# Binary cross-entropy on one core: loading the next predictions ahead of the store

## Chip, cores and metric

The kernel runs on one core of a Trainium2 chip. The metric is device time in microseconds. Three runs of the kernel before took 1864.36, 1864.77 and 1865.55 us; the median is 1864.77.

## What is computed

```python
def reference(pred, target):          # both 8192 x 8192 float32
    eps = 1e-7
    pred = np.clip(pred, eps, 1 - eps)
    return -(target * np.log(pred) + (1 - target) * np.log(1 - pred))
```

The targets are 0 or 1, drawn as integers and kept as float32. So each output is -ln(pred) where the target is 1 and -ln(1 - pred) where it is 0. Every element is independent. 268.44 MB of predictions and as many of targets are read, and 268.44 MB are written.

## The kernel before

With targets of 0 or 1 the two logarithms are one: |target - 1 + pred| is pred where the target is 1 and 1 - pred where it is 0. A chunk of w columns on 128 partitions therefore takes these steps, in place on one buffer of predictions:

- `clip` (line 88, VectorE): bound the predictions to [eps, 1 - eps].
- `log` (lines 94, 97, 98): VectorE computes (target - 1) + pred, ScalarE takes the absolute value (97) and then the logarithm (98).
- `back` (line 102, VectorE): multiply by -1.
- `load_p` (line 72) and `load_t` (line 75) are the loads of predictions and targets, `store` (line 79) writes the result.

The work is cut into 40 chunks: two of 5120 columns at the start (0 and 1), 35 of 14336 columns (2 to 36), two of 5632 and one of 1024 at the end (37 to 39, called a, b and c). Predictions live in a ring of three slots of 14336 columns: chunks 0 and 1 share the first slot, chunk 2 has the second, chunk 3 the third, chunk 4 the first again, and so on. So the load of predictions k+2 overwrites the slot from which store k-1 reads, and has to wait until that store has landed. (Predictions 3 are the first of the third slot and wait for nothing; predictions 4 wait for stores 0 and 1.) Targets are turned from float32 to bfloat16 by the load and live in one single buffer, so the load of targets k+1 waits until VectorE has read the last of targets k (line 94, second half). Chunk c has places of its own in both buffers.

The order of the instructions on each engine is the written one; there is no scheduler. Chunks 2 to 36 are computed in two halves. VectorE's order in a round of chunk k is clip and line 94 of the first half, the same of the second half, then `back` of both halves; each `back` waits for ScalarE.

All loads but that of predictions 0, and all stores but the last three chunks', are issued by GpSimd (POOL) and go through one queue. An instruction that waits on POOL holds up all that is behind it. In a round of the middle POOL issues targets k+1 (line 75), store k (line 79) and predictions k+2 (line 72), in this order. The start issues targets 0 and 1 and predictions 1 and 2 with no wait, predictions 0 come by ScalarE's queue; the stores of a, b and c go by SyncE's queue.

Of the kernel before, what the change touches and what calls it, by code (L numbers as in the profile page):

```python
# [1 line left out]

# [4 lines left out]

EPS = 1e-7

BIG = 14 * 1024  # L10
FIRST = 5 * 1024
LAST = 5632
TAIL = 1024
SLOTS = 3


def plan(total):
    n = (total - 2 * FIRST - 2 * LAST - TAIL) // BIG
    assert n > 4 and total == 2 * FIRST + n * BIG + 2 * LAST + TAIL
    spots = [(FIRST, 0, 0), (FIRST, FIRST, FIRST)]  # L20
    spots += [(BIG, k % SLOTS * BIG, 0) for k in range(1, n + 1)]
    end = (n + 1) % SLOTS * BIG
    spots += [(LAST, end, 0), (LAST, end + LAST, LAST)]
    return spots + [(TAIL, SLOTS * BIG, BIG)]


@with_exitstack
def kernel(
    ctx: ExitStack,
    tc: tile.TileContext,  # L30
    pred: bass.AP,
    target: bass.AP,
    out: bass.AP,
):
    nc = tc.nc
    fp32 = mybir.dt.float32
    bf16 = mybir.dt.bfloat16
    Alu = mybir.AluOpType
    Act = mybir.ActivationFunctionType
    P = nc.NUM_PARTITIONS  # L40

    R, C = pred.shape
    spots = plan(R * C // P)
    n = len(spots)
    widths = [s[0] for s in spots]
    cols = [sum(widths[:k]) for k in range(n)]

    def chunk(ap, k):
        flat = ap.rearrange("r c -> (r c)")
        return flat[cols[k] * P : (cols[k] + widths[k]) * P].rearrange("(p w) -> p w", p=P)  # L50

    pool = ctx.enter_context(tc.tile_pool(name="rings", bufs=1))
    ring_p = pool.tile([P, SLOTS * BIG + TAIL], fp32, name="ring_p", tag="ring_p")
    ring_t = pool.tile([P, BIG + TAIL], bf16, name="ring_t", tag="ring_t")
    warm = pool.tile([1, 8], fp32, name="warm", tag="warm")

    def spot(k, part=(0, 1)):
        w, c, _ = spots[k]
        i, m = part
        return ring_p[:, c + i * w // m : c + (i + 1) * w // m]  # L60

    def spot_t(k, part=(0, 1)):
        w, _, c = spots[k]
        i, m = part
        return ring_t[:, c + i * w // m : c + (i + 1) * w // m]

    def load_p(k):
        if k == 0:
            for rows in (slice(0, P, 2), slice(1, P, 2)):
                nc.scalar.dma_start(out=spot(0)[rows], in_=chunk(pred, 0)[rows])  # L70
        else:
            nc.gpsimd.dma_start(out=spot(k), in_=chunk(pred, k))  # L72

    def load_t(k):
        nc.gpsimd.dma_start(out=spot_t(k), in_=chunk(target, k))  # L75

    def store(k):
        queue = nc.sync if k >= n - 3 else nc.gpsimd
        queue.dma_start(out=chunk(out, k), in_=spot(k))  # L79

    def store_rows(k):
        src, dst = spot(k), chunk(out, k)
        for first, last in ((0, 108), (108, 120), (120, 128)):
            nc.sync.dma_start(out=dst[first:last], in_=src[first:last])

    def clip(k, *part):
        p = spot(k, *part)
        nc.vector.tensor_scalar(  # L88
            out=p, in0=p, scalar1=EPS, scalar2=1 - EPS, op0=Alu.max, op1=Alu.min
        )  # L90

    def log(k, *part):
        p = spot(k, *part)
        nc.vector.scalar_tensor_tensor(  # L94
            out=p, in0=spot_t(k, *part), scalar=1.0, in1=p, op0=Alu.subtract, op1=Alu.add
        )
        nc.scalar.activation(out=p, in_=p, func=Act.Abs)  # L97
        nc.scalar.activation(out=p, in_=p, func=Act.Ln)  # L98

    def back(k, *part):  # L100
        p = spot(k, *part)
        nc.vector.tensor_scalar(out=p, in0=p, scalar1=-1.0, scalar2=None, op0=Alu.mult)  # L102

    with tc.manual_schedule():
        nc.vector.memset(warm, 1.0)  # L105
        load_t(0)
        load_p(0)
        load_t(1)
        load_p(1)
        load_p(2)  # L110
        nc.scalar.activation(out=warm, in_=warm, func=Act.Ln)  # L111
        for k in (0, 1):
            clip(k)
            log(k)
        load_t(2)
        back(0)
        store(0)
        back(1)
        store(1)
        load_p(3)  # L120
        a, b, c = range(n - 3, n)
        for k in range(2, n - 3):
            for h in (0, 1):
                clip(k, (h, 2))
                log(k, (h, 2))
            if k < n - 4:
                load_t(k + 1)
            else:
                load_t(a)
                load_t(b)  # L130
                load_p(c)
                load_t(c)
                back(k, (0, 2))
                for j in (a, b):
                    clip(j)
            if k < n - 4:
                back(k, (0, 2))
            back(k, (1, 2))
            store(k)
            if k + 2 < n - 3:  # L140
                load_p(k + 2)
            elif k + 2 == n - 3:
                load_p(a)
                load_p(b)
        log(a, (0, 2))
        log(a, (1, 2))
        clip(c)
        log(b, (0, 2))
        back(a, (0, 2))
        log(b, (1, 2))  # L150
        back(a, (1, 2))
        store(a)
        log(c)
        back(b, (0, 2))
        back(b, (1, 2))
        store(b)
        back(c)
        store_rows(c)


# [1 line left out]
_INS = ['pred', 'target']  # L162
_OUTS = [((8192, 8192), 'float32')]


# [23 lines left out]
```

## Time and profile before

| what | value |
|---|---|
| median of 3 runs | 1864.77 us (1864.36 to 1865.55) |
| span of the profiled execution | 1863.3 us (its own time outside the profile is not recorded) |
| busy VectorE (DVE) | 1121.6 us, 60% |
| busy ScalarE (ACT) | 902.4 us, 48% |
| busy GpSimd (POOL), issues of DMAs | 178.7 us, 10% |
| POOL's DMA queue, share of 16 engines | 99.0% |
| a prediction load, a store, a target load of 14336 columns, median from issue to landing | 44.3, 31.1, 31.3 us |
| mean time of POOL's issues: lines 72, 75, 79 | 561, 724, 3459 ns |

"Idle before" in the profile is the time that an engine stood still just before an instruction, with what ended it. The chain that ended last follows the last instruction back to what released it. The time from issue to landing counts from the start of the instruction on POOL to the moment that all its data is in place, so it contains the time that a transfer stands in the queue behind others. Sizes of the loads of targets are given as they arrive, in bfloat16; from memory twice as much is read.

### The profile page before, as it was taken

The numbers are of one execution on the slowest core, as the hardware profiler recorded it, in microseconds if no ns is written. First come the engines' busy times: TensorE is split into PE (matmuls) and PEld (weight loads), VectorE is DVE, ScalarE is ACT, GpSimd is POOL, SyncE is SP. The second block draws the span as 40 slices with busy tenths as digits, with TensorE's granted clock in tenths as the row PEclk, the third lists the DMA queues.
The fourth block names the chain that finished last, engine by engine and source line by source line (L and its number), as shares of the span: only waits on it lengthen the run. The fifth ranks groups of instructions, "written<-read, shape, count | busy, mean of one in ns | idle before, by whom it ended". The sixth has DMA issues, their size and how long they took to land.

```text
span 1863.3 us, 713 instructions
## 1 busy us (share of the span) xinstructions
DVE 1121.6 (60%) x230; ACT 902.4 (48%) x156; POOL 178.7 (10%) x120
## 2 busy tenths in 40 slices
DVE  4666555555666566655555666566655555666565
ACT  4454444455555544444445555544444445555554
POOL 1111101111110011101111110011101111110020
DMA  9999999999999999999999999999999999999999
GB/s 344 348 370 356 355 356 355 355 355 355 357 375 374 374 372 355 355 355 355 355 355 355 359 374 374 375 375 361 355 355 356 356 356 355 356 367 374 374 353 352
DMA packets 17318, 671.15 MB, mean 360 GB/s; under 512 B 1952, under 2 KB 1952, under 8 KB 2336
## 3 DMA queue, kind: packets, MB, share of 16 engines
q0 software_dynamic: 16704, 662.18, 99.0%
q1 hardware_dynamic: 448, 6.29, 0.8%
q10 hardware_dynamic: 160, 2.62, 0.4%
q14 instruction: 6, 0.05, 0.0%
HBM read 536.87 MB, written 268.44 MB: 432 GB/s over the span
## 4 chain that ended last, share of the span: by engine, by line
DMA 60%; issue 35%; ACT 3%; DVE 1%; POOL 0%; POOLq 0%; DVEq 0%; PEldq 0%
DMA ring_t<-in_target_dram 58%; DMA ring_p<-in_pred_dram 2%; ACT ring_p L98 1%; ACT ring_p L97 1%; DVE ring_p L94 1%; DVE ring_p L102 0%; POOL out_dram L79 0%; DVE ring_p L88 0%; POOL ring_t L75 0%; POOLq L75 0%; POOL ring_p L72 0%; POOLq L79 0%; DVEq L94 0%; PEldq L184 0%
## 5 line engine op out<-in xcount | busy, mean ns | idle before, releaser
L97 ACT ACTIVATE ring_p<-ring_p 128x7168 f32<-128x7168 f32 (+3 forms) x77 | 452.0, 5870 | 940.7 <-DVE ring_p L94 940.7
L94 DVE SCALAR_TENSOR_TENSOR ring_p<-ring_t,ring_p 128x7168 f32<-128x7168 bf16 (+3 forms) x77 | 558.2, 7251 | 372.0 <-DMA ring_t<-in_target_dram 370.7
L102 DVE TENSOR_SCALAR ring_p<-ring_p 128x7168 f32<-128x7168 f32 (+3 forms) x77 | 285.4, 3707 | 329.4 <-ACT ring_p L98 329.4
L98 ACT ACTIVATE ring_p<-ring_p 128x7168 f32<-128x7168 f32 (+3 forms) x77 | 452.6, 5877 | 2.4
L88 DVE TENSOR_SCALAR ring_p<-ring_p 128x7168 f32<-128x7168 f32 (+3 forms) x75 | 284.6, 3794 | 24.4 <-DMA ring_p<-in_pred_dram 24.4
L79 POOL DMA_DIRECT2D out_dram<-ring_p x37 | 128.0, 3459 | 584.4 <-DVE ring_p L102 584.2
L75 POOL DMA_DIRECT2D ring_t<-in_target_dram x40 | 29.0, 724 | 1057.2 <-DVE ring_p L94 1056.4
L72 POOL DMA_DIRECT2D ring_p<-in_pred_dram x39 | 21.8, 561 | 2.5 <-issue 2.5
L111 ACT ACT_TABLE_LOAD x1 | 1.3, 1283 | 1.9 <-issue 1.9
L105 DVE MEMSET warm<- 1x8 f32 x1 | 0.1, 65 | 0.8 <-PEq L173 0.8
L111 ACT ACTIVATE warm<-warm 1x8 f32<-1x8 f32 x1 | 0.2, 208 | 0.0
L173 POOL MEMSET const-float32-0.0<- 128x1 f32 x1 | 0.1, 99 | 0.2 <-issue 0.2
L173 POOL MEMSET const-bfloat16-1.0<- 128x1 bf16 x1 | 0.1, 102 | 0.0
L173 POOL MEMSET const-uint8-127<- 128x1 uint8 x1 | 0.1, 100 | 0.0
L173 POOL MEMSET const-float32-1.0<- 128x1 f32 x1 | 0.1, 99 | 0.0
## 6 DMA issues: line engine op xcount, KB each, us to landing
ring_p<-in_pred_dram POOLq DMA_DIRECT2D x35, 7168.0 KB, 44.3
out_dram<-ring_p POOLq DMA_DIRECT2D x35, 7168.0 KB, 31.1
ring_t<-in_target_dram POOLq DMA_DIRECT2D x35, 3584.0 KB, 31.3
ring_p<-in_pred_dram POOLq DMA_DIRECT2D x2, 2816.0 KB, 37.1
out_dram<-ring_p SPq DMA_DIRECT2D x2, 2816.0 KB, 14.6
out_dram<-ring_p POOLq DMA_DIRECT2D x2, 2560.0 KB, 27.9
ring_t<-in_target_dram POOLq DMA_DIRECT2D x2, 1408.0 KB, 26.5
ring_p<-in_pred_dram ACTq DMA_DIRECT2D x2, 1280.0 KB, 10.5
```

The lines of the kernel that those rows point to most:

```text
L72: nc.gpsimd.dma_start(out=spot(k), in_=chunk(pred, k))
L75: nc.gpsimd.dma_start(out=spot_t(k), in_=chunk(target, k))
L79: queue.dma_start(out=chunk(out, k), in_=spot(k))
L88: nc.vector.tensor_scalar(out=p, in0=p, scalar1=EPS, scalar2=1 - EPS, op0=Alu.max, op1=Alu.min)
L94: nc.vector.scalar_tensor_tensor(out=p, in0=spot_t(k, *part), scalar=1.0, in1=p, op0=Alu.subtract, op1=Alu.add)
L97: nc.scalar.activation(out=p, in_=p, func=Act.Abs)
L98: nc.scalar.activation(out=p, in_=p, func=Act.Ln)
L102: nc.vector.tensor_scalar(out=p, in0=p, scalar1=-1.0, scalar2=None, op0=Alu.mult)
L105: nc.vector.memset(warm, 1.0)
L111: nc.scalar.activation(out=warm, in_=warm, func=Act.Ln)
L173: nc = _bacc.Bacc("TRN2", target_bir_lowering=False, num_devices=1)
```

## The change

In each round the load of predictions k+2 is issued ahead of store k instead of behind it: targets k+1, predictions k+2, store k. In the round of chunk 35 the loads of a's and b's predictions, which take the place of predictions k+2, move in the same way. In the start, the load of predictions 3 moves from behind stores 0 and 1 to the place right behind targets 2. The order on VectorE and ScalarE stays, in the last big chunk (36) too, where the branches are only written in another way. The waits follow the data as before: predictions k+2 still wait for store k-1.

```diff
         load_t(2)
+        load_p(3)
         back(0)
         store(0)
         back(1)
         store(1)
-        load_p(3)
         a, b, c = range(n - 3, n)
         for k in range(2, n - 3):
             for h in (0, 1):
...
                 log(k, (h, 2))
             if k < n - 4:
                 load_t(k + 1)
+                if k + 2 < n - 3:
+                    load_p(k + 2)
+                else:
+                    load_p(a)
+                    load_p(b)
             else:
                 load_t(a)
                 load_t(b)
                 load_p(c)
                 load_t(c)
-                back(k, (0, 2))
+            back(k, (0, 2))
+            if k == n - 4:
                 for j in (a, b):
                     clip(j)
-            if k < n - 4:
-                back(k, (0, 2))
             back(k, (1, 2))
             store(k)
-            if k + 2 < n - 3:
-                load_p(k + 2)
-            elif k + 2 == n - 3:
-                load_p(a)
-                load_p(b)
```

## The prediction

> **What bounds the kernel now.** I read the page first: engines, the slices, the DMA queues, the chain that ended last. Then the groups and the issues, then the timeline of one round in the middle, then the list of the chain's pieces for the length of every round.
>
> From the page of before:
>
> ```profile
> span 1863.3 us, 713 instructions
> DVE 1121.6 (60%) x230; ACT 902.4 (48%) x156; POOL 178.7 (10%) x120
> DMA  9999999999999999999999999999999999999999
> q0 software_dynamic: 16704, 662.18, 99.0%
> HBM read 536.87 MB, written 268.44 MB: 432 GB/s over the span
> DMA 60%; issue 35%; ACT 3%; DVE 1%; POOL 0%; POOLq 0%; DVEq 0%; PEldq 0%
> ring_p<-in_pred_dram POOLq DMA_DIRECT2D x35, 7168.0 KB, 44.3
> out_dram<-ring_p POOLq DMA_DIRECT2D x35, 7168.0 KB, 31.1
> ring_t<-in_target_dram POOLq DMA_DIRECT2D x35, 3584.0 KB, 31.3
> ```
>
> The reader should see one full resource: the transfers of POOL's queue fill 99.0% of the DMA engines' time, in every slice, while DVE has 60% and ACT 48%. The chain that ended last says "DMA 60%; issue 35%", which looks like a wait for the issue of targets; the timeline shows that it is not one. One round of it (start, us, engine, line):
>
> ```profile
> 465.94 7.62 DVE L94 SCALAR_TENSOR_TENSOR ring_p<-ring_t,ring_p 128x7168 f32<-128x7168 bf16 x1 [10.72 <-DMA ring_t<-in_target_dram]
> 473.48 3.89 DVE L88 TENSOR_SCALAR ring_p<-ring_p 128x7168 f32<-128x7168 f32 x1
> 477.40 7.63 DVE L94 SCALAR_TENSOR_TENSOR ring_p<-ring_t,ring_p 128x7168 f32<-128x7168 bf16 x1
> 485.32 0.53 POOL L75 DMA_DIRECT2D ring_t<-in_target_dram  x1 [29.47 <-DVE ring_p L94]
> 498.29 3.89 DVE L102 TENSOR_SCALAR ring_p<-ring_p 128x7168 f32<-128x7168 f32 x1 [8.38 <-ACT ring_p L98]
> 502.10 3.88 DVE L88 TENSOR_SCALAR ring_p<-ring_p 128x7168 f32<-128x7168 f32 x1
> 502.48 3.63 POOL L79 DMA_DIRECT2D out_dram<-ring_p  x1 [16.62 <-DVE ring_p L102]
> 506.10 0.53 POOL L72 DMA_DIRECT2D ring_p<-in_pred_dram  x1
> 516.70 7.62 DVE L94 SCALAR_TENSOR_TENSOR ring_p<-ring_t,ring_p 128x7168 f32<-128x7168 bf16 x1 [10.71 <-DMA ring_t<-in_target_dram]
> ```
>
> ```profile
> 434.56 31.29 DMA ring_t<-in_target_dram
> 485.32 31.28 DMA ring_t<-in_target_dram
> ```
>
> Call the chunk that DVE takes up at 465.94 k. Its targets landed at 434.56 + 31.29 = 465.85, the next ones land at 485.32 + 31.28 = 516.60: a round is 50.75 us (in the chain's pieces the 32 rounds from 109.8 to 1734.25 lie between 50.63 and 51.11, median 50.74). Landings inside the round, by the medians of the issues: store k-1 at 451.71 + 31.1 = 482.8, predictions k+1 at 455.33 + 44.3 = 499.6, targets k+1 at 516.6. So one transfer ends every 16.9 us, one behind the other, and 3 x 16.9 is the round. Targets are 3584 KB in SBUF but are read as 7168 KB, so all three move the same bytes on the memory side: 22.02 MB in 50.74 us is 434 GB/s, the page's 432 over the span. The targets issued at 485.32 wait for the transfer of predictions to end at 499.6; that is a margin of 14 us and not a stall. Every issue is early in this sense, so the end is set by bytes.
>
> **Part 1, the round (in 34 rounds the loads of predictions move ahead of a store; the last of them are a's and b's).** Bytes, transfers, DVE and ACT instructions and their order stay; on POOL's queue t, s, p becomes t, p, s. If the queue never runs dry, the round stays 3 x 16.9 us. So each issue must be shown to be early in the new order:
> - New landings: predictions k+1 at 482.8, store k-1 at 499.7, targets k+1 at 516.6. DVE still starts chunk k at 465.9, so its times above hold.
> - Targets k+1: issued at 485.3 as before, needed when store k-1 ends near 499.7, less the tail of its landing (at most about 2, one packet: 57 KB at 434/16 GB/s is 2.1 us). Margin 12 us.
> - Predictions k+2 get a new wait. They overwrite the slot of store k-1, and that landed long before in the old order (482.8 against the issue at 506.10). Now POOL waits until 499.7. In that time DVE runs two TENSOR_SCALARs without a break, 498.29 to 502.18 and 502.10 to 505.98. The row at 502.48 shows what such an instruction does to an issue: 3.63 us, ending with DVE's, where the same store at 40.04, beside other work, took 0.54. So the issue ends at 500.3 at best and at 506.1 at worst. It is needed when targets k+1 end, near 514.5: margin 8 to 14 us. Cost 0.
> - Store k is queued behind this wait on POOL. It is ready at 502.2 (end of the negation L102), so it is issued by 506.1 to 506.7 instead of 502.5 to 506.1. Its turn now comes only after predictions k+2, near 531: margin 25. Behind it POOL has targets k+2 at 536, which wait for DVE as before.
> - DVE's clip of k+1 at 502.10 now finds predictions landed 19 us before rather than 2.5. DVE is not the bound; gain 0. Cover for all this is the transfer of targets k+1 (16.9 us); without it the new wait would cost about 1 to 6.4 us in each of 34 rounds, 34 to 218 us.
>
> At this place the Trainium skill ("SBUF — State Buffer", section "SBUF: two separate sides") has a rule that speaks against the change: a DMA issued from GpSimd has its descriptors written by GpSimd, which is shut out of the shared port while VectorE runs a two-port instruction, and the DMA engines then sit idle. The 3.63 us against 0.54 agrees with the first half. Taken by itself the rule would charge the block of 6.4 us to each round (1863.3 + 218); by the rows the engines have 8 us of targets left, and the sum is 0.
>
> **Part 2, the start.** Predictions 3 go to a free slot and are issued right behind targets 2 instead of behind store 1: at 40.4 instead of 52.8. At that time the engines work on predictions 2, and targets 2 land at 63.4 in both. Before: stores 0 and 1 (6.0 us each at 434 GB/s) and predictions 3 follow, then targets 3, which land at 109.8. After: predictions 3, stores 0 and 1, targets 3, the same sum, so again 109.8. Store 0 goes out at 40.9 instead of 40.04, store 1 at 49.2 as before; both wait behind predictions 3 until 80. Targets 3 are issued at 82.87 and needed near 90: margin 7. Predictions 4 need both stores landed, near 92.4, and are needed near 107: margin 14. Gain or loss 0. The start had no hole to fill: the page's first slices are 9 and the first 63.5 us have a DMA share of 0.98.
>
> **Part 3, the end.** The loads of a and b (6.6 us each) pass store 35. After targets 36 land at 1785.0, both orders run the same bytes. Targets a are issued at 1792.93 and are needed near 1815; the margin is larger than before. DVE waited 3.25 us for b's predictions at 1815.26; that goes, and ScalarE is late next (its L98 ends at 1817.33), so store 36 is issued 0.9 us earlier than 1822.44. The engines reach that store only near 1829, and from there to the end they have a share of 0.9 to 1.0. Bounds of this part: 0 and -0.9; I take 0, since the end has no gap to move into.
>
> **Unknown: what a boundary between two transfers costs.** No row shows predictions behind targets or a store behind predictions. Bound: targets 2 to targets 3 took 46.41 us for 19.92 MB in four transfers, a round 50.74 for 22.02 MB in three. Solved for a rate and a price for each transfer, that is 444 GB/s and 0.4 us. If the new neighbours took one boundary away or doubled one, 34 rounds would change by 14 us down or up. The cyclic order has in both cases one load behind a load, one store behind a load, one load behind a store, so the nearest value is 0. I take 0.
>
> **Sum.** 1863.3 + 0 + 0 + 0 = 1863.3 us of span. The profiled execution's own time is not shown beside its span; the three runs have a median of 1864.77, so 1.5 us lie around. Forecast 1864.8.
>
> **Rivals.**
> 1. Boundaries get dearer: the new neighbours (store behind predictions, targets behind a store) cost half a boundary, 0.2 us, more in 34 rounds: 1864.8 + 6.8 = 1871.6. For it: two rounds of 32 took 51.11 us, so something in a transfer varies. Against: the other 30 stay within 0.3 us.
> 2. Boundaries get cheaper by the same: 1858.0. This is the other side. Place: the change from store to load, price 0.2 us a round; it decides (over 0.2%, 3.7 us) from 0.11 us a round on, which is the distance of the fastest round from the median. Against: the kinds of boundary are the same in number.
> 3. The queue runs dry: predictions k+2 come too late behind their new wait. It decides if the issue takes 8 us longer than 506.1. One us beyond costs 34 us: about 1899. For it: the block by DVE is real and falls just there. Against: DVE is idle from 505.98 to 516.70, so the block must end.
> 4. The change does not do what it says: the order of instructions on POOL is the written one, with the waits above, so I give it nothing of its own.
>
> **Chances.** No change 0.76; rival 1 0.11; rival 2 0.09; rival 3 0.04. About 0.2% is what a measurement of this kernel can tell from no change, so faster 0.09, within 0.76, slower 0.15. The range from 1860 to 1870 holds the first case and the smaller half of the first two rivals; rival 3 and the ends of 14 us are left out. The likeliest case by itself is 1863 to 1867.
>
> **What would show it.** In the profile after: targets still land 50.7 us apart; q0 stays at 99%; the median to landing of stores goes from 31.1 up to about 44 and that of predictions from 44.3 down to 27 to 33 (if the issue is stamped at its start, after the wait); POOL L72 waits for a DMA in each round or is stretched to some us, and L79 shrinks; DVE's wait for b's predictions is gone. Wrong if rounds are longer than 50.9 or shorter than 50.6 throughout, or if DVE's wait for targets (10.7 us a round) grows.

## The result and the profile after

The changed kernel takes 1870.53 us (median of 6 runs, 1869.71 to 1871.29) against 1864.83 us: a ratio of 1.0029, interval 1.0019 to 1.0039. It is 5.7 us slower. The forecast was no change, 1864.8, with a range to 1870; the time lies half a microsecond above the range, in the direction of rival 1. The profiled execution of the new kernel took 1871.29 us, its span 1869.5.

The page after, with the lines that answer to those of before (busy times, the queue, the chain that ended last, POOL's groups, the three big transfers with their medians to landing):

```profile
span 1869.5 us, 713 instructions
DVE 1122.0 (60%) x230; ACT 902.4 (48%) x156; POOL 231.9 (12%) x120
q0 software_dynamic: 16704, 662.18, 98.8%
HBM read 536.87 MB, written 268.44 MB: 431 GB/s over the span
DMA 61%; DVE 36%; ACT 1%; issue 1%; POOL 0%; DVEq 0%; PEldq 0%
L72 POOL DMA_DIRECT2D ring_p<-in_pred_dram x39 | 77.7, 1994 | 485.7 <-DMA out_dram<-ring_p 483.2
L79 POOL DMA_DIRECT2D out_dram<-ring_p x37 | 125.1, 3382 | 29.1 <-DVE ring_p L102 23.4
ring_p<-in_pred_dram POOLq DMA_DIRECT2D x35, 7168.0 KB, 33.7
out_dram<-ring_p POOLq DMA_DIRECT2D x35, 7168.0 KB, 48.2
ring_t<-in_target_dram POOLq DMA_DIRECT2D x35, 3584.0 KB, 31.4
```

The change did what it says. Predictions (L72) now wait 483.2 us in all for stores, and their issues are stretched from 561 to 1994 ns by VectorE's instructions. A store takes 48.2 us to landing instead of 31.1, a load of predictions 33.7 instead of 44.3. Work and bytes are the same. The queue is still full, 98.8% against 99.0%. VectorE's wait for targets, whose growth the prediction named as a sign of being wrong, has grown by 5.5 us in all. Its group before, then after:

```profile
L94 DVE SCALAR_TENSOR_TENSOR ring_p<-ring_t,ring_p 128x7168 f32<-128x7168 bf16 (+3 forms) x77 | 558.2, 7251 | 372.0 <-DMA ring_t<-in_target_dram 370.7
L94 DVE SCALAR_TENSOR_TENSOR ring_p<-ring_t,ring_p 128x7168 f32<-128x7168 bf16 (+3 forms) x77 | 558.2, 7251 | 377.5 <-DMA ring_t<-in_target_dram 376.2
```

One round in the timeline of the kernel after:

```profile
568.82 7.63 DVE L94 SCALAR_TENSOR_TENSOR ring_p<-ring_t,ring_p 128x7168 f32<-128x7168 bf16 x1 [10.67 <-DMA ring_t<-in_target_dram]
588.20 0.53 POOL L75 DMA_DIRECT2D ring_t<-in_target_dram  x1 [29.94 <-DVE ring_p L94]
603.66 1.53 POOL L72 DMA_DIRECT2D ring_p<-in_pred_dram  x1 [14.93 <-DMA out_dram<-ring_p]
605.36 3.63 POOL L79 DMA_DIRECT2D out_dram<-ring_p  x1 [0.18 <-issue]
620.34 7.62 DVE L94 SCALAR_TENSOR_TENSOR ring_p<-ring_t,ring_p 128x7168 f32<-128x7168 bf16 x1 [11.46 <-DMA ring_t<-in_target_dram]
```

Predictions were issued by 605.2, 15 us before the targets ahead of them had landed on the last DMA engine and 10 us before they had on the first (by the landing events explained below), so the new wait itself is covered. Yet this round took 51.5 us. Pieces of the chain after show how uneven the rounds have become (start and length of the wait for targets):

```profile
486.38 31.62 DMA ring_t<-in_target_dram
537.47 31.26 DMA ring_t<-in_target_dram
588.20 32.04 DMA ring_t<-in_target_dram
639.72 31.28 DMA ring_t<-in_target_dram
```

Their ends lie 50.73, 51.51 and 50.76 us apart. Over the whole kernel: targets 3 land at 109.0 (before 109.8), targets 36 at 1789.9 (before 1785.0), the span ends at 1869.5 (before 1863.3). The start gained 0.8 us, the 33 rounds lost 5.7, the end 1.3.

**Where in a round.** Each transfer is shared by the 16 DMA engines. The trace has 16 landing events for each transfer, with their times; they are taken here as one for each engine. The time of the last minus that of the first is called the lag below. This is worked out from the landing events of the trace. For targets 36, the 16 engines' landings, in us behind the first:

```
before 0 .01 .05 .06 .17 .25 .28 .29 .58 .70 .98 1.72 2.64 2.70 2.73 2.99
after  0 .06 .13 .20 .23 .35 .42 .47 1.29 1.71 6.55 7.04 7.10 7.19 7.24 7.91

                 first engine  last engine
before           50.732        50.751       us a round, targets 5 (at 211 us) to 36
after            50.732        50.922
```

The first engines run at the same pace in both kernels. A few fall back, by 3 us before and 8 us after, and more so early on (after: 6.3 us by targets 20, 1.6 more in the 16 rounds behind); what waits for a transfer waits for the last engine. By targets 3 this lag was 2.05 us before and 1.23 after, so in the 33 rounds it grew by 0.9 and by 6.7 us: the difference, 5.7 us, is the loss in the rounds. The packets of the big transfers (128 to a transfer, one row of the tile each) tell where it arises: most take 2.12 to 2.13 us. Over 2.2 us were 55 of 13440 before and 121 after, 17.8 and 48.3 us of excess over all engines. Matched with the landings, 53 of the 55 and 114 of the 121 are the last packet that an engine moves of a load that stands ahead of a store. That load is the targets in the old order, the predictions in the new. I call this place the turn, and time it by the slowest engine's landing of that load.

### The profile page after: what moved, and what is told of

Read it like the earlier page. It is cut to its first block, busy times and chain, and to the rows that moved or that the text cites. A ratio compares the mean times of both kernels' runs of the same rounds, so it can differ in the third digit from the quotient of the medians.

```text
span 1869.5 us, 713 instructions
## 1 busy us (share of the span) xinstructions
DVE 1122.0 (60%) x230; ACT 902.4 (48%) x156; POOL 231.9 (12%) x120
## 3 DMA queue, kind: packets, MB, share of 16 engines
q0 software_dynamic: 16704, 662.18, 98.8%
## 4 chain that ended last, share of the span: by engine, by line
DMA 61%; DVE 36%; ACT 1%; issue 1%; POOL 0%; DVEq 0%; PEldq 0%
DMA ring_t<-in_target_dram 60%; DVE ring_p L94 29%; DVE ring_p L88 7%; DMA ring_p<-in_pred_dram 1%; ACT ring_p L98 1%; ACT ring_p L97 1%; POOL ring_t L75 0%; DVEq L94 0%; DVE ring_p L102 0%; PEldq L183 0%
## 5 line engine op out<-in xcount | busy, mean ns | idle before, releaser
L72 POOL DMA_DIRECT2D ring_p<-in_pred_dram x39 | 77.7, 1994 | 485.7 <-DMA out_dram<-ring_p 483.2
## 6 DMA issues: line engine op xcount, KB each, us to landing
ring_p<-in_pred_dram POOLq DMA_DIRECT2D x35, 7168.0 KB, 33.7
out_dram<-ring_p POOLq DMA_DIRECT2D x35, 7168.0 KB, 48.2
```

## Experiments

Each comparison is with runs of the kernel before on the same chip. The expectations number the theories: 1 is what stands ahead of the store, 2 the work of VectorE and ScalarE beside the turn, 3 the new wait, 4 the start, 5 to 8 conditions on the time of issues, formed as the earlier ones fell.

### The two halves of the change

`start_only`:

```diff
         load_t(2)
+        load_p(3)
         back(0)
...
         store(1)
-        load_p(3)
```

> Only the start is changed: predictions 3 are loaded ahead of stores 0 and 1; the rounds keep targets, store, predictions. Theory 1 (the last load packets ahead of a store are slowed, and full-width predictions more than targets that are cast on the way; the loss comes once a round): rounds stay at 50.75 us, time within 1 us of before (1864.8). Theory 2 (the turn from load to store now falls into the work of VectorE and ScalarE): same as before. Theory 3 (the new wait of the load on the store leaves the queue short): same as before, as the wait is not there. Theory 4 (the start costs it): the whole 5.7 us, 1870.5.

`rounds_only` has the rest of the change:

```diff
         load_t(2)
-        load_p(3)
         back(0)
...
         store(1)
+        load_p(3)
```

(against the new kernel)

> Only the rounds are changed, the start is that of before. Theories 1, 2 and 3: 1870.5, rounds of 50.9 us on average. Theory 4 (the start): 1864.8.

Measured: the start alone 1865.12 us (ratio 1.0001, 0.9991 to 1.0010), last engine 50.762 us a round, lag at the end 3.3 us. The rounds alone 1871.05 (1.0031, 1.0019 to 1.0044), 50.945 us a round, lag 8.0 us. The order in the rounds is the whole loss; theory 4 falls.

### Without the work on the chunks

Both copies leave clip, log and back out, so they store the predictions as they are:

```diff
+    def nothing(k, *part):
+        pass
+
+    clip = log = back = nothing
+
     with tc.manual_schedule():
```

> All work of VectorE and ScalarE on the chunks is left out (the output is the predictions as they are); the DMAs and their order are those of before. All theories: still set by the transfers, 50.75 us a round, within 2 us of 1864.8, less what the work in the start and the end costs (up to 5 us).

> The same without work on the chunks, in the new order of the DMAs. Theory 2 (the work of VectorE and ScalarE beside the turn from load to store): equal to the copy in the old order within 1 us. Theories 1 and 3: again 4 to 7 us longer than the copy in the old order, slowest engine's rounds 50.9 us.

Measured: the copy in the old order 1873.09 us (ratio 1.0040, 1.0025 to 1.0055), last engine 51.016 us a round, lag 10.7 us; the copy in the new order 1870.40 (1.0027, 1.0016 to 1.0038), 50.778 us a round, lag 3.2 us. Their totals also have another start and end, so the rounds are what counts. Without the work it is the old order that loses. No theory had that: the neighbours are the same with and without work, so theory 1 can't be all, and theory 2 had the copies equal. What the work changes for the transfers is when they are issued.

### The same transfers in the same order, issued early or late

The new order, with targets k+1 loaded in two halves of the columns. `split_early` has the first half first; `split_late` the second:

```diff
-                load_t(k + 1)
+                load_t(k + 1, (0, 2))     # split_late: (1, 2)
+                load_t(k + 1, (1, 2))     # split_late: (0, 2)
```

> New order, but in the rounds the targets are loaded in two halves, the second half of the columns first, so that both halves are issued where the whole was (19.4 us after the targets landed); predictions still stand ahead of the store. What the copies left open is why the slowest engines lose time in one order with the work and in the other without it. Theory 1 (predictions ahead of a store cost more than targets): as the new order, 1870 to 1872, slowest engines 7 to 8 us behind the first at the end. Theory 5 (the loss at the turn from load to store stays small when POOL issues a new transfer while the load ahead of the store runs, and grows when it issues none in that time: none in the new order, none in the copy of the old one; some in the old order and in the copy of the new one): also 1870 to 1872. One more transfer a round may cost up to 2 us in all.

> The same transfers of half the targets, but first half first: each is issued as soon as VectorE has read that half, about 1 us before and 11 us after the targets landed, which is while the predictions ahead of the store are loaded. Theory 1: as with the halves the other way round, 1870 to 1872, lag 7 to 8 us. Theory 5: 1864 to 1867, lag about 3 us.

The issues of POOL in one round, first `split_late`, then `split_early` (L77 is targets, L72 predictions, L81 the store):

```profile
858.96 1.75 POOL L72 DMA_DIRECT2D ring_p<-in_pred_dram  x1 [10.52 <-DMA out_dram<-ring_p]
860.89 3.64 POOL L81 DMA_DIRECT2D out_dram<-ring_p  x1 [0.17 <-issue]
895.12 4.70 POOL L77 DMA_DIRECT2D ring_t<-in_target_dram  x2 [30.60 <-DVE ring_p L96]
```

```profile
855.77 0.53 POOL L72 DMA_DIRECT2D ring_p<-in_pred_dram  x1 [22.66 <-DMA out_dram<-ring_p]
856.29 0.54 POOL L81 DMA_DIRECT2D out_dram<-ring_p  x1
871.90 3.63 POOL L77 DMA_DIRECT2D ring_t<-in_target_dram  x1 [15.07 <-DVE ring_p L96]
883.37 0.53 POOL L77 DMA_DIRECT2D ring_t<-in_target_dram  x1 [7.84 <-DVE ring_p L96]
```

The transfer that ends before L72 is released is a store; then come 17 us of targets and 17 us of predictions, so the turn is 34 us behind: by the landing events at 892.6 and at 889.3. `split_late` issues the next targets 2.5 us after its turn, `split_early` issues the two halves 17 and 6 us before.

Measured: `split_late` 1871.31 us (1.0030, 1.0019 to 1.0041), lag 6.5; `split_early` 1866.43 (1.0002, 0.9993 to 1.0011), lag 2.7. The first engines need 50.78 us a round in both, 0.05 more than with whole targets: that is the price of one more transfer, 1.6 us in 34 rounds. Order and transfers are equal but for which half of the columns comes first, and 4.9 us lie between them. So not what stands ahead of the store decides, but when the transfers behind it are issued. Theory 1 falls; theory 5 was met here. Theory 3 falls too: `split_early` has the new wait (22.66 us in the row of L72) and loses next to nothing.

### Half the targets on each side of the predictions, and a shorter old order

`split_tpts`:

```diff
-                load_t(k + 1)
+                load_t(k + 1, (0, 2))
                 if k + 2 < n - 3:
                     load_p(k + 2)
                 else:
                     load_p(a)
                     load_p(b)
+                load_t(k + 1, (1, 2))
```

> First half of the targets, predictions, second half of the targets, store: predictions are ahead of the store, but the store comes behind cast targets. Theory 1: 1864 to 1867, lag about 3 us. Theory 3 (the new wait of predictions on the store costs the time): the wait is still there and holds up half of the targets too, so 1870 or more. Theory 5: the store is issued while targets and predictions run and the first half of the next targets about 17 us before the second has landed, so the load ahead of the store sees no issue or one at its edge: 1867 to 1871.

Measured 1871.59 us (1.0032, 1.0022 to 1.0042), but lag only 2.4: here all engines lose, the first need 50.917 us a round. Predictions and the second half are issued once the store has landed, when only the first half (8.5 us) is left to run. I read this as the old theory 3, in a kernel where the cover of the new wait was halved; no run separates it further. It isn't what happens in the change, where the first engines keep their 50.73 us.

`short_before` is the old order without clip and without ScalarE's activations:

```diff
-        nc.scalar.activation(out=p, in_=p, func=Act.Abs)
-        nc.scalar.activation(out=p, in_=p, func=Act.Ln)
...
+    def clip(k, *part):
+        pass
+
     with tc.manual_schedule():
```

> Old order, but the clip on VectorE and both activations on ScalarE are left out, so that the store and the next predictions are issued about 24 us after the targets landed, 6 us before the load ahead of the store begins, where the old kernel issues them 40 us after, in the middle of that load. Theories 1 and 3: as before, rounds of 50.75 us, lag 3 us. Theory 2 (work beside the turn): as before, since no work ran there. Theory 5: rounds of 50.9 to 51.0 us, lag 7 us or more, 1869 to 1873 less up to 4 us for the shorter end.

Measured 1865.39 us (0.9998, 0.9989 to 1.0007), 50.776 us a round, lag 3.6. Store and predictions were issued 27 us before the turn, none while the load ahead of the store ran, and nothing was lost. Theory 5 falls in that form.

### Which issue matters

The three next runs keep work and big transfers whole. `late_store_after` holds the store back until the targets have landed; `act` and `add` are the parts of `log` with explicit columns, `negate` is `back`:

```diff
-            for h in (0, 1):
-                clip(k, (h, 2))
-                log(k, (h, 2))
+            clip(k, (0, 2))
+            add(k, 0, 64)
+            if k > 2:
+                negate(k - 1, BIG - 64, BIG)
+                store(k - 1)
+            add(k, 64, BIG // 2)
+            act(k, (0, 2))
+            clip(k, (1, 2))
+            log(k, (1, 2))
...
-            back(k, (1, 2))
-            store(k)
+            if k < n - 4:
+                negate(k, BIG // 2, BIG - 64)
...
```

> New order. The last 64 columns of a chunk are negated only once the next targets have landed, so the store is issued about 0.5 us after they landed instead of 11 us before: 14 us ahead of its turn instead of 25. The issue of targets stays at 19.4 us after the landing, so nothing stands in the queue behind the store when the engines come to it. Theory 6 (the slowest engines lose time when nothing stands behind the store in the queue as they turn from load to store): as the new order, 1870 to 1872, lag 6 to 8 us. Theory 7 (they lose time when the last issue before the turn was more than about 24 us ago): 1865 to 1867, lag 3 us. Theory 8 (they lose time when a transfer is issued within 10 us after the turn, as in the new order, the halves issued late and the copy in the old order): 1870 to 1872.

Measured 1871.25 us (1.0034, 1.0021 to 1.0047), lag 6.8. The moment of the store's own issue doesn't matter; theory 7 falls.

`filler_after` puts a small load behind each store:

```diff
+    def filler(k):
+        nc.gpsimd.dma_start(out=scratch, in_=chunk(pred, k)[:16, :128])
...
             store(k)
+            if k < n - 4:
+                filler(k)
```

> New order, and behind each store a small load of 16 rows of 512 bytes into a buffer of its own is issued, at once after the store. Then something stands in the queue behind the store; all other issues stay where they are. Theory 6: 1865 to 1867.5 (the small loads cost up to 2 us), lag 3 us. Theories 7 and 8: 1870 to 1873, lag 6 to 8 us.

Measured 1869.79 us (1.0026, 1.0016 to 1.0036), lag 5.9; the small load costs all engines 0.03 us a round, 1 us in all. A small transfer behind the store takes away little of the lag, so theory 6 as it stood (anything behind the store) falls. Left is the narrower form, that it must be a big transfer.

`late_load_before` is the old order, predictions k+2 held back until the next targets have landed:

```diff
+            add(k, 0, 64)
+            if 2 < k < n - 4:
+                nc.vector.memset(spot(k + 1)[:, :8], 0.0)
+                load_p(k + 1)
...
+            add(k, 64, BIG // 2)
...
             store(k)
-            if k + 2 < n - 3:
-                load_p(k + 2)
```

> Old order, but predictions k+2 are held back until the targets of the next chunk have landed (VectorE first writes 8 columns of their slot), about 2.5 us after the engines' turn to the store instead of 8 us before it. Now nothing stands behind the store at the turn. Theory 6: lag 6 us or more, 1868 to 1872. Theory 7: as the old order, 1864.5 to 1866, lag 3 us. Theory 8: as theory 6.

Measured 1869.70 us (1.0035, 1.0021 to 1.0049). The old order now loses 5.0 us as well. Its profile is of one execution that took 1877.72 us, the slowest, in which the first engines too lost time (50.909 us a round). But they did so only in its last rounds: up to targets 27 they kept 50.7 us, and by then the lag had already grown to 9.9 us, against 3.0 in the kernel before.

### An issue at the turn, with a transfer behind the store

`filler_before` is the old order with a small load issued just after the turn:

```diff
+    def filler(k):
+        nc.vector.memset(scratch, 0.0)
+        nc.gpsimd.dma_start(out=scratch, in_=chunk(pred, k)[:16, :128])
...
+            add(k, 0, 64)
+            if k > 2:
+                filler(k)
+            add(k, 64, BIG // 2)
```

> Old order, predictions k+2 stand behind the store as before; in addition a small load of 16 rows of 512 bytes is issued in each round about 0.5 us after the targets landed, 2.5 us after the slowest engines' turn to the store. Theory 8 (an issue within 10 us after the turn makes the slowest engines fall back): lag 6 us or more, 1869 to 1872. Theory 6 in its narrower form (no whole transfer behind the store at the turn makes them fall back): lag 3 us, 1864.5 to 1867.

Measured 1867.50 us (1.0012, 1.0003 to 1.0021), lag 5.0. The small load as a transfer is about 1 us of the 2.1; the lag grew by 2 us, less than theory 8 had, more than theory 6 had. Neither is met.

`split_mid` is `split_early` with the second half issued later:

```diff
...
+            clip(k, (1, 2))
             if k < n - 4:
-                load_t(k + 1)
+                add(k, BIG // 2, BIG - 64)
...
+                load_t(k + 1, (0, 2))
+                back(k, (0, 2))
+                add(k, BIG - 64, BIG)
+                act(k, (1, 2))
+                load_t(k + 1, (1, 2))
...
```

> New order, targets in two halves, the first issued about 16 us before the turn as in the run with both halves early, the second only about 1 us after the turn (VectorE takes the last 64 columns after the negation of the first half). Theory 6, narrower: half of the targets stands behind the store, so lag 3 to 4 us, 1866 to 1868. Theory 8: lag 6 us or more, 1869 to 1872.

Measured 1868.59 us (1.0018, 1.0008 to 1.0027), lag 3.8. With half of the targets in the queue before the turn the lag stays small, though half of them is issued at the turn. That is what theory 6 in the narrower form had for the lag; the time is 0.6 us above its range.

`later_load_before` moves `late_load_before`'s issue behind the whole of line 94:

```diff
             add(k, 0, 64)
+            add(k, 64, BIG // 2)
             if 2 < k < n - 4:
                 nc.vector.memset(spot(k + 1)[:, :8], 0.0)
                 load_p(k + 1)
-            add(k, 64, BIG // 2)
```

> Old order, predictions k+2 held back as in the run that held them until the targets landed, but until 8 us after the landing, 10 us after the turn. Theory 6, narrower: nothing stands behind the store at the turn, lag 6 us or more, 1868 to 1872. Theory 8: the issue moves to the edge of its 10 us, so the lag is clearly below the 9.5 us of the earlier issue, 3 to 6 us.

Measured 1899.07 us (1.0179, 1.0162 to 1.0196), far from both. The timeline of this kernel shows why the issue came later than intended:

```profile
882.46 7.69 DVE L110 SCALAR_TENSOR_TENSOR ring_p<-ring_t,ring_p 128x64 f32<-128x64 bf16 x2 [11.42 <-DMA ring_t<-in_target_dram]
890.08 3.88 DVE L88 TENSOR_SCALAR ring_p<-ring_p 128x7168 f32<-128x7168 f32 x1
890.10 0.07 DVE L146 MEMSET ring_p<- 128x8 f32 x1
890.47 3.62 POOL L72 DMA_DIRECT2D ring_p<-in_pred_dram  x1 [19.32 <-DVE ring_p L146]
```

The issue fell under VectorE's clip and took 3.62 us, as the Trainium skill's page "SBUF — State Buffer", section "SBUF: two separate sides", has it for descriptors written by GpSimd. It ended at 894.09; the first engines landed the store at 896.5, the last at 899.3. So it was just in time, and the engines were not left without work: in the window of the rounds the DMA share is 1.00 (before 1.01). But packets became slower. 586 of the 4480 target packets took over 2.2 us, now on all 16 engines, and nearly all of them are again the last ones before the store. The first engines need 51.72 us a round and the lag stays at 4. These packets make up 24 of the 31 us of excess over the usual packet time per engine, and they are over when the targets have landed (882.4 in this round), 8 us before the round's late issue begins. So most of what was lost wasn't lost in waiting for that issue. Why all engines fall back here, and only some in `late_load_before`, where nothing big stood behind the store either, stays open.

### What the runs say together

The "next issue" is timed from the slowest engine's landing of the load ahead of the store. The last column is the difference of the medians.

| kernel | order | big transfer behind the store at the turn | next issue after the turn | lag at the end | us against before |
|---|---|---|---|---|---|
| before | t, s, p | predictions | 19 us | 3.0 | 0 |
| start_only | t, s, p | predictions | 19 us | 3.3 | +0.2 |
| short_before | t, s, p | predictions | 15 us | 3.6 | -0.2 |
| split_tpts | half t, p, half t, s | half the targets | 17 us | 2.4 | +6.0 (all engines lose) |
| split_early | t, p, s | targets | 17 us | 2.7 | +0.8 |
| copy_after | t, p, s | targets | 17 us | 3.2 | start and end differ |
| split_mid | t, p, s | half the targets | 0 us, half the targets | 3.8 | +3.2 |
| later_load_before | t, s, p | none | 8 us | 4.0 | +33.7 (all engines lose) |
| filler_before | t, s, p | predictions | 0.7 us, small | 5.0 | +2.1 |
| filler_after | t, p, s | small | 2.5 us | 5.9 | +5.1 |
| split_late | t, p, s | none | 2.5 us | 6.5 | +5.7 |
| late_store_after | t, p, s | none | 3 us | 6.8 | +6.6 |
| after | t, p, s | none | 2.5 us | 7.9 | +5.7 |
| rounds_only | t, p, s | none | 2.5 us | 8.0 | +6.1 |
| late_load_before | t, s, p | none | 0.6 us | 9.5 (its slowest execution) | +5.0 |
| copy_before | t, s, p | predictions | 0.3 us, targets and store | 10.7 | start and end differ |

Shown: the order of the transfers by itself doesn't set the time. The new order runs at nearly the old pace when the targets are in the queue at the turn, and loses 5 us or more when they come just after it. In the old order it was the predictions, issued right behind the store and 10 us before the turn, that stood there. In the new order the predictions have become the load ahead of the store, and what stands behind the store is the next targets, which can't be issued before VectorE has read the last of the present ones.

Open: what in a DMA engine makes the last packet ahead of a store longer. "A big transfer behind the store" fits most lags of the table: at most 3.8 us with one there, or half of one, and 5.9 or more without. Three do not fit: `filler_before` (5.0 with predictions there), `later_load_before` (4.0 with nothing there, but all engines lost), and the copy in the old order, which has predictions there and the largest lag; it also is the only one that issues two big transfers at the very turn. "No issue at the turn" fits that one, but not `split_mid`, and `filler_before` only in part. The order in time speaks against it besides: the long packets end with the turn, and in all kernels of the table but `split_mid` the next issue begins only behind it, in the copy 0.3 us after the slowest engine's landing. So an issue after the turn can't have made the packets of the same round longer. The two conditions weren't separated further. Nor was it settled why the lag stops growing: near 3 us before, near 8 after, and at 10.7 from targets 24 on in the copy in the old order.

A version faster than both was not found: before, the last engine is 3.0 us behind the first at the end of the rounds, so no more than that is to be gained in the lag.

## Why the prediction was wrong

- **What bounds the kernel** was right: bytes through one full queue, 99% before and 98.8% after; VectorE's and ScalarE's busy times are the same within 0.4 us.
- **Part 1, the new wait** was right in its working. Predictions are released by the store's landing, their issue takes 1.5 to 2.4 us beside VectorE's instruction, and they are in the queue 14 to 16 us before the last engine's turn. The forecast margin was 8 to 14. Seen from the first engine it is smaller than forecast in the end, as the lag eats it: 14.6 us in the first round, 6.4 in the last. It sufficed, since the first engines keep 50.732 us a round in both kernels; so rival 3 (a late issue) is not what happened. The issue that `later_load_before` made late cost 33.7 us, one us a round, but with the queue not empty and mostly in packets that had ended before it, so by another mechanism than rival 3's.
- **"Cost 0" for the round rested on "if the queue never runs dry, the round stays 3 x 16.9 us".** This step failed. It took the 16 engines as one. A queue that is full for all of them is not the same as 16 engines that keep pace: each engine's round lies between 50.73 and, for the slowest, 50.92 us, and the round ends with the slowest. Between the kernels the last engine's round grew by 0.17 us on average (50.92 against 50.75), over all 33 rounds by 5.7 us.
- **The unknown, a boundary's price,** was bounded at 14 us up and down and then taken as 0, since "the kinds of boundary are the same in number". The number is the same, but the same boundary costs more or less with what stands in the queue at that moment. Rival 1 had the place (the turn to the store, and dearer) and nearly the size, 6.8 us, with a chance of 0.11; its reason, the new neighbour, fell with `split_early`, so that its size came out near is luck. The 0.4 us for each transfer was far too high: one more transfer a round cost 0.05 us. The two rounds of 51.11 us before, noted as "something in a transfer varies", were this loss in its first rounds: in each of them the lag grew by 0.35 us or more, from 2.05 to 2.40 and from 2.46 to 2.83.
- **The start:** targets 2 were to land at 63.4 in both and landed at 62.3. The 16 longer packets at the first turn to a store, which stood between 59.0 and 60.0 in the old kernel (2.3 to 3.1 us each), moved to 75.8 with the predictions. By targets 3 the new kernel was 0.8 us ahead, and `start_only` shows that nothing of it is left at the end.
- **The end:** VectorE's wait for b's predictions is gone, as forecast, and the store of chunk 36 was still early. The 1.3 us that the end takes longer were not examined; its DMA share is 0.92 against 0.96.
- **The Trainium skill's rule** ("SBUF — State Buffer", section "SBUF: two separate sides"), that GpSimd's issue is shut out while VectorE runs a two-port instruction, agrees with the rows as far as the issue goes (0.54 against 3.63 us). That the DMA engines then sit idle did not come about here: the cover that the forecast set against it was there.

## What to carry to other kernels

A queue at 99% says that the engines are busy, not that they keep pace with each other; look at the 16 landings of one transfer, early and late in the run, before calling a reorder of equal bytes free. When transfers change places, ask for each turn from load to store what is already issued behind it, and try to keep a big transfer there: it went with the smaller lags here, with two exceptions. The issue to move forward is then the one that comes just after the turn: here the targets loaded in halves, each as soon as its half had been read, cost 4.9 us less than the same halves loaded at the turn.

## What was not expected of the hardware

- DMA engines that work from the same full queue drift apart and stay apart: lags of 2.4 to 10.7 us at the end of the rounds, while the first ones kept 50.73 us a round in the kernel before, after, and in five of the experiments that left the three big transfers whole.
- The last packet of a load ahead of a store is the one that grows, from 2.12 to as much as 3.2 us in the new kernel, while nearly all others stay within 0.02 us.
- With the load behind the store issued 8 us after the turn, in time for the engines by 2.4 us, all 16 engines had long last packets ahead of the store and lost 1 us a round, though the DMA share stayed at 1.00 (`later_load_before`).
